# Second parts of the weights on VectorE in the first mixing, and fixed places for the sums in the second

## The chip, the core and the metric

The kernel runs on one core of a Trainium2 chip. The metric is the device time of one execution in microseconds (us): the median of several runs. A profile of one execution goes with it.

## The reference

One layer of a hybrid decoder is applied to a prompt (2048 tokens) and to 8 short samples (8 tokens each, with states from earlier tokens). Both share the weights; the model width is 1024.

```python
h = rmsnorm(x, norm_mix_w)
rq, rk, rv, rg, hq, hf, hi, hg = split(h @ w_in)              # 8 parts of 4 heads x 128
o_r = retention(rotary(rq), rotary(rk), rv)                    # 4 heads, fixed decay per head
f   = lb + (1 - lb) * sigmoid(hf)                              # 4 heads, decay per channel
o_h = gated_recurrence(silu(hq), 1 - f, hi, log(f))
o   = concat(head_rmsnorm(o_r) * silu(rg), head_rmsnorm(o_h) * silu(hg))
x   = x + o @ w_out
x   = x + square(relu(rmsnorm(x, norm_ffn_w) @ w_up)) @ w_down # inner width 4096
y   = rmsnorm(x, final_norm_w)
```

All values are float32; the states after the last token are outputs too.

## The kernel before

The tokens are worked through in three groups of 512, 832 (the 64 sample tokens and 768 of the prompt) and 768 columns. Each group passes through a mixing (input projection and recurrence of four heads), the output projection and the feed-forward part. "First mixing" is `mix` of group 0, "second mixing" that of group 1. The features lie on the 128 partitions, the tokens along the free dimension.

**Split float32.** TensorE multiplies in a reduced format (fp32r). Each float32 operand is therefore cut in two: a first part `hi`, made on ScalarE by a copy that rounds, and a second part `lo = raw - hi`. A product takes three matmuls: hi x hi, hi x lo, lo x hi.

**Weights.** `plan_stream` lists all weight tiles (128 x 1024) in the order of use. `weight(i)` runs when tile i is needed, and prepares the tiles up to i + 2: it loads `raw` (two buffers) on the SP queue, casts `hi` on ScalarE (line 277) and has `second_part` (line 292) make `lo`. Until the change line 280 chooses the engine: entries of the first 40 tiles, which are those of group 0's input and output projection, go to GpSimd (POOL) at once if their number is over 3 and not a multiple of 4, which are 27 tiles; the others go to VectorE, 4 ticks later. Tiles of the feed-forward part of groups 1 and 2 carry a third field, which chooses the engine there. In group 0, `next_weight` stores both parts in DRAM from tile 4 on (line 325); groups 1 and 2 load these, so they make no second parts in their mixing but for the first four tiles.

**Order of the work.** Instructions are issued by a clock of ticks: a tick follows each step of the matmul loops (`tick`). `later(n, f)` issues f n ticks on. The mixer of a head (`mixer`) is such a list of ticks: logs, scans, then for six widths the exponents (lines 832, 833 on POOL), their exponential (line 837 on ScalarE) and the decayed queries and keys (843, 844 on VectorE); scores in PSUM that are copied into a tile `AT` (lines 857, 877, 900 on VectorE, 916 on ScalarE); retention scores (lines 970, 971); column sums (504, 505) of parts cut by lines 359 and 360; transposes (788, copied by 790 and 792). Projections leave PSUM through lines 639 and 702 on VectorE. Small PSUM tiles share four buffers named `mm`, the projections' two named `pj`. The framework also orders instructions of one engine by when their operands are ready.

**Heads.** In group 1 a head's projections take 4 x 24 ticks, its values 56, and the gates of a head 2 x 24, the gates coming ahead of the next head's projections or at the end. So the mixer of a head starts after ticks 96, 296, 496 and 696 of the mixing, and the mixing ends after tick 800. The output projection takes 192 ticks more.

**Sums of weights.** The feed-forward part of groups 1 and 2 multiplies 2 x 2 blocks by seven products instead of eight and so needs sums of weight blocks. `plan_sums` makes them on the side: a set loads four tiles (A21, A22, A11, A12, tag `sum`, four buffers) at 0, 0, 12 and 24 ticks from its start, makes four additions on VectorE (line 1293) at 40, 50, 60 and 70, and stores the results at 60, 70, 80 and 90 (line 1298). Seven sets (for w_up) are made in group 0's feed-forward part, eight (for w_down) in the second mixing. What is left of them is issued by a loop `while self.side`. Their loads and stores, like all DMAs named here, are on the SP queue.

Of the kernel before, what the change touches and what calls it, by code (L numbers as in the profile page):

```python
# [41 lines left out]
W_UP0 = W_OUT0 + N_OUT  # L42
W_DN0 = W_UP0 + N_UP
NQ = FF // (4 * P)
NO = NQ // 2
# [162 lines left out]
class Kernel:  # L208
# [43 lines left out]
    def weight(self, i):  # L252
        n = len(self.stream)
        while self.w_next < min(i + 1 + self.ahead, n):
            j = self.w_next
            e = self.stream[j]
            if e[0] == "p":

                self.wts[j] = tuple(self.wp.tile([P, WT], F32R, tag=tag, name=tag) for tag in ("hi", "lo"))
                for part, kept in zip(self.wts[j], self.kept[e[1]]):  # L260
                    self.nc.sync.dma_start(part.bitcast(F32), kept)
                self.w_next += 1
                self.w_load = max(self.w_load, j + 1)
                continue
            while self.w_load <= j or j >= self.n_first and self.w_load <= j + 2 and self.w_load < n:
                if self.stream[self.w_load][0] == "p":
                    break
                k, later = self.w_load, self.w_load >= self.n_first
                raw = self.raws[k] = self.wp.tile([P, WT], F32, tag="sum" if later and k % 3 else "raw", name="raw",
                                                  bufs=4 if later and k % 3 else 2)  # L270
                e = self.stream[k]
                self.fetch(raw, self.sums[e[1]] if e[0] == "s" else self.I["w"][e[1]])
                self.w_load += 1
            raw = self.raws.pop(j)
            hi = self.wp.tile([P, WT], F32R, tag="hi", name="hi")
            lo = self.wp.tile([P, WT], F32R, tag="lo", name="lo")
            self.nc.scalar.copy(hi, raw)  # L277
            self.wts[j] = (hi, lo)
            self.second[j] = raw
            pool = self.stream[j][2] if len(self.stream[j]) > 2 else j % 4 and 3 < j < W_UP0  # L280
            if pool or j < 4:
                self.second_part(j, self.nc.gpsimd if pool else self.nc.vector)
            else:
                self.later(4, self.second_part, j, self.nc.vector)
            self.w_next += 1
        self.second_part(i, self.nc.vector)
        return self.wts[i]
# [91 lines left out]
    def build(self):  # L379
        nc, tc, I = self.nc, self.tc, self.I  # L380
        with ExitStack() as ctx:
            cp = ctx.enter_context(tc.tile_pool(name="cp", bufs=1))
            self.wp = ctx.enter_context(tc.tile_pool(name="wp", bufs=3))
            self.sl = ctx.enter_context(tc.tile_pool(name="sl", bufs=NSLAB))
            self.ld = ctx.enter_context(tc.tile_pool(name="ld", bufs=NLD))
            self.small = ctx.enter_context(tc.tile_pool(name="small", bufs=2))
            self.pj = ctx.enter_context(tc.tile_pool(name="pj", bufs=2, space=bass.MemoryType.PSUM))
            self.pm = ctx.enter_context(tc.tile_pool(name="pm", bufs=4, space=bass.MemoryType.PSUM))
            self.dp = ctx.enter_context(tc.tile_pool(name="dp", bufs=1, space=bass.MemoryType.DRAM))
            self.w_next = self.w_load = self.w_use = 0  # L390
            self.n_mm = self.n_ticks = 0
            self.raws, self.sums, self.side = {}, {}, deque()
            self.ordered, self.spread, self.n_proj = True, False, 0
            self.ahead = 2
            self.wts, self.second, self.kept = {}, {}, {}
            self.blocks = deque()
            self.plan_stream()

            con = cp.tile([P, NCONST], F32, name="con")
            vec = cp.tile([P, NVEC], F32, name="vec")  # L400
            msk = cp.tile([P, 2 * NLV, P], U8, name="msk")
            self.ones = cp.tile([P, P], F32, name="ones")
            self.ones_r = cp.tile([P, P], F32R, name="ones_r")
            nc.vector.memset(self.ones, 1.0)
            nc.vector.tensor_copy(self.ones_r, self.ones)
            eps = cp.tile([P, 2], F32, name="eps")
            nc.vector.memset(eps[:, 0:1], EPS)
            nc.vector.memset(eps[:, 1:2], EPS * DK)
            self.eps, self.eps_h = eps[:, 0:1], eps[:, 1:2]
            self.con, self.vec, self.msk = con, vec, msk  # L410
            self.ident = con[:, C_ID:C_ID + P]

            gs = []
            off = 0
            for ns, p0, n in GROUPS:
                g = type("G", (), {})()
                g.i, g.ns, g.p0, g.n, g.T, g.off = len(gs), ns, p0, n, ns + n, off
                off += g.T
                nch = n // C
                first = nch // 2  # L420
                g.pieces = [(0, g.T)] if g.T <= 512 else [(0, g.T // 2), (g.T // 2, g.T)]
                g.segs = [list(range(first)), list(range(first, nch))]
                gs.append(g)
            nc.scalar.dma_start(vec, I["vec"])
            nc.scalar.preload_act_table_set("natural_log_exp_and_others")
            self.norm_in(gs[0], True)
            self.ahead = 2
            self.weight(0)

            self.reset = cp.tile([P, P + NS], F32, name="reset")  # L430
            nc.gpsimd.memset(self.reset, 1.0)
            nc.gpsimd.memset(self.reset[:, P:].rearrange("p (c t) -> p c t", t=SLEN)[:, :, 0:1], 0.0)
            self.S = cp.tile([P, 2 * H, P], F32, name="S")
            self.AT = [cp.tile([P, 3, P], F32, name=f"AT{i}") for i in range(2)]
            for a in self.AT:
                nc.gpsimd.memset(a, 0.0)
            self.ATs = cp.tile([P, P], F32, name="ATs")
            nc.gpsimd.memset(self.ATs, 0.0)
            self.lower_bounds(cp)

            sums = [(("u", t), W_UQ0 + 4 * t) for t in range(1, NQ)]
            sums += [(("d", o, v), W_DQ0 + 4 * (2 * o + v)) for o in range(NO) for v in range(2)]
            for i, g in enumerate(gs):
                nxt = gs[i + 1] if i + 1 < len(gs) else None
                if i == 0:
                    self.mix(g)
                    self.plan_sums(sums[:NQ - 1], 90, 200)

                    self.spread = True
                    self.out_proj_first(g)  # L450
                    self.ffn_first(g, nxt)
                    self.spread = False
                    continue
                if i == 1:
                    self.finish_first(gs[0])
                    self.plan_sums(sums[NQ - 1:], 100, 84)
                else:
                    self.finish(gs[i - 1])
                self.mix(g)
                while self.side:  # L460
                    self.side.popleft()[1]()
                self.out_proj(g)
                self.ffn(g, nxt)
            nc.sync.dma_start(self.O["ret_p"].rearrange("h d v -> d h v"), self.S[:, :H])
            nc.sync.dma_start(self.O["hg_p"].rearrange("h d v -> d h v"), self.S[:, H:])
# [814 lines left out]
        self.later(4 * KB + 10, factor)  # L1280


    def plan_sums(self, sets, first, every):
        nc, w = self.nc, self.I["w"]
        self.side = deque()

# [10 lines left out]
            s = self.sums[key + (name,)] = self.dp.tile([P, WT], F32, name="s" + "".join(map(str, key)) + name)  # L1297
            self.tc.keep_in_program_order(nc.sync.dma_start(s, x[name]))

        for j, (key, i) in enumerate(sets):  # L1300
            x, t = {}, self.n_ticks + first + every * j
            steps = [(0, load, x, i, "A21", "A22"), (12, load, x, i, "A11"), (24, load, x, i, "A12"),
                     (40, make, x, "S1", "A21", ALU.add, "A22", "A22"),
                     (50, make, x, "S3", "A11", ALU.subtract, "A21", "A21"),
                     (60, make, x, "S2", "S1", ALU.subtract, "A11", "A11"),
                     (70, make, x, "S4", "A12", ALU.subtract, "S2", "A12")]
            steps += [(d, keep, x, key, name) for d, name in ((60, "S1"), (70, "S3"), (80, "S2"), (90, "S4"))]
            for d, fn, *a in sorted(steps, key=lambda z: z[0]):
                self.side.append((t + d, lambda fn=fn, a=a: fn(*a)))
# [463 lines left out]
```

## Time and profile before

| what | value |
|---|---|
| median of 3 runs | 2588.03 us (2586.77 to 2589.51) |
| profiled execution, its own time | 2586.12 us |
| its span, first to last instruction | 2584.3 us |
| mean granted TensorE clock | 0.997 |
| DMA | 442.33 MB, mean 171 GB/s |
| first mixing | about 30 to 300 us |
| second mixing | about 680 to 1110 us |

The profile's lines give engine (PE is TensorE, PEld its weight loads, DVE is VectorE, ACT ScalarE, POOL GpSimd), line of the kernel, operation, names of the tiles written and read, and times. In a timeline, the bracket at the end of a row is the time for which the engine was idle before it, and the instruction that ended the wait.

### The profile page before, as it was taken

The page shows a single profiled execution, that of the slowest core. Times are in us where ns is not written, and L with a number is a line of the kernel's source. Part 1 is how long each engine was busy: PE and PEld are TensorE (multiplying, and loading weights), DVE is VectorE, ACT ScalarE, POOL GpSimd, SP SyncE. Part 2 cuts the span into 40 slices and gives each one's busy share as a digit, 9 for nine tenths or more (in the row PEclk, how much of TensorE's full clock was granted, in tenths as well). Part 3 has the DMA queues.
Part 4 walks back from the last instruction along what each step waited for, and adds up shares of the span by engine and source line. Part 5 has one row for each costly group of instructions (what it writes and reads, how often), then busy time and mean ns, then how long its engine had stood idle before and what let it go on. Part 6 is the DMA issues. An engine that isn't in the chain of part 4 may idle for free. (4 is left out here: it accounts for less than half of the span.)

```text
span 2584.3 us, 37190 instructions
## 1 busy us (share of the span) xinstructions
PE 2538.6 (98%) x14689; PEld 2404.1 (93%) x14689; DVE 1688.4 (65%) x2122; ACT 1166.5 (45%) x1575; POOL 772.3 (30%) x480
## 2 busy tenths in 40 slices
PE   8999999999999999999999999999999999999997
PEld 6888788888999999999999999999999999999997
DVE  6666776556666576646655977875556465559886
ACT  6666533234434343345434444454444354345443
POOL 5655251111234143201222322242244012223222
PEclk9999999999999999999999999999999999999999
DMA  7556755554264655613456555442222325565452
GB/s 256 207 201 210 279 202 195 192 195 161 98 220 158 225 202 170 230 72 136 167 169 228 206 174 177 149 160 82 99 108 100 120 90 179 183 218 194 171 180 82
DMA packets 146237, 442.33 MB, mean 171 GB/s; under 512 B 14736, under 2 KB 36240, under 8 KB 146064
## 3 DMA queue, kind: packets, MB, share of 16 engines
q1 hardware_dynamic: 145920, 439.94, 48.8%
q8 instruction: 116, 1.90, 0.3%
q14 instruction: 57, 0.47, 0.1%
q10 hardware_dynamic: 144, 0.02, 0.0%
HBM read 331.11 MB, written 108.79 MB: 170 GB/s over the span
## 5 line engine op out<-in xcount | busy, mean ns | idle before, releaser
L352 PE MATMUL pj<-slab,hi 128*128 128x416 f32 (+2 forms) x2844 | 742.4, 364 | 6.3 <-ACT hi L277 5.9
L277 ACT CAST hi<-raw 128x1024 fp32r<-128x1024 f32 x330 | 346.7, 1051 | 677.9 <-PE pu L1145 191.6
L292 POOL TENSOR_TENSOR lo<-raw,hi 128x1024 fp32r<-128x1024 f32 x119 | 314.7, 2645 | 933.9 <-ACT hi L277 866.4
L352 PEld LDWEIGHTS pj<-slab,hi 128*128 128x128 f32 x2844 | 514.3, 189 | 39.1 <-ACT hi L277 5.9
L1145 PE MATMUL pd<-slab,hi 128*128 128x416 f32 (+1 forms) x1792 | 469.5, 342 | 5.1 <-DVE slab L1588 3.1
L352 PE MATMUL pj<-slab,lo 128*128 128x416 f32 (+2 forms) x1422 | 435.6, 364 | 0.1
L1145 PE MATMUL pu<-slab,hi 128*128 128x416 f32 (+1 forms) x1600 | 408.1, 342 | 0.0
L292 DVE TENSOR_TENSOR lo<-raw,hi 128x1024 fp32r<-128x1024 f32 x211 | 269.5, 1277 | 188.7 <-ACT hi L277 188.2
L1145 PEld LDWEIGHTS pd<-slab,hi 128*128 128x128 f32 x1792 | 329.4, 188 | 8.7 <-DVE slab L1588 3.7
L1145 PE MATMUL pd<-slab,lo 128*128 128x416 f32 (+1 forms) x896 | 307.9, 344 | 0.0
L1145 PEld LDWEIGHTS pu<-slab,hi 128*128 128x128 f32 x1600 | 294.0, 188 | 1.5
L352 PEld LDWEIGHTS pj<-slab,lo 128*128 128x128 f32 x1422 | 259.9, 189 | 17.2 <-issue 1.9
L1145 PE MATMUL pu<-slab,lo 128*128 128x416 f32 (+1 forms) x800 | 264.2, 343 | 0.0
L352 PE MATMUL mm<-slab,hi 128*128 128x512 f32 x740 | 229.5, 390 | 0.0
L727 PE MATMUL pjv<-hi,slab 128*128 128x256 f32 x1088 | 211.9, 286 | 1.0 <-ACT slab L737 1.0
L1344 DVE TENSOR_TENSOR slab<-slab 128x832 fp32r<-128x832 f32 (+1 forms) x144 | 162.9, 1148 | 37.4 <-ACT slab L1340 18.1
L727 PEld LDWEIGHTS pjv<-hi,slab 128*128 128x128 f32 x1088 | 174.2, 190 | 3.0 <-ACT slab L737 1.4
L1340 ACT CAST slab<-slab 128x832 fp32r<-128x832 f32 (+1 forms) x144 | 122.0, 860 | 116.7 <-DVE slab L1351 83.1
L1145 PEld LDWEIGHTS pd<-slab,lo 128*128 128x128 f32 x896 | 168.1, 188 | 0.5
L352 PEld LDWEIGHTS mm<-slab,hi 128*128 128x128 f32 x740 | 138.5, 188 | 29.2 <-ACT slab L1175 0.4
L727 PE MATMUL pjv<-lo,slab 128*128 128x256 f32 x544 | 153.8, 283 | 0.0
L1145 PEld LDWEIGHTS pu<-slab,lo 128*128 128x128 f32 x800 | 149.7, 188 | 0.5
(205 smaller groups left out, 3708.3 us busy)
## 6 DMA issues: line engine op xcount, KB each, us to landing
raw<-w SPq DMA_DIRECT2D x270, 512.0 KB, 4.1
u<-ld SPq DMA_DIRECT2D x32, 416.0 KB, 4.2
slab<-u SPq DMA_DIRECT2D x32, 416.0 KB, 5.7
u<-ld SPq DMA_DIRECT2D x32, 384.0 KB, 4.6
slab<-u SPq DMA_DIRECT2D x32, 384.0 KB, 4.9
ld<-x SPq DMA_DIRECT2D x16, 416.0 KB, 4.8
ld<-x SPq DMA_DIRECT2D x16, 384.0 KB, 4.0
raw<-su1S SPq DMA_DIRECT2D x8, 512.0 KB, 3.9
```

The costliest lines, as they stand in the source:

```text
L277: self.nc.scalar.copy(hi, raw)
L292: eng.tensor_tensor(out=lo, in0=self.second.pop(j), in1=hi.bitcast(F32), op=ALU.subtract)
L352: self.nc.tensor.matmul(pj[:, i, :T2], w, a[:, c0:c1], start=j == 0 and q == 0, stop=j == n - 1 and q == 2)
L727: nc.tensor.matmul(pj[:, i * 256:(i + 1) * 256], a[:, s:s + C], ww, start=kb == 0 and q == 0, stop=kb == KB - 1 and q == 2)
L1145: self.nc.tensor.matmul(*a, **k)
L1340: self.nc.scalar.copy(hi[:, :g.T], B[name][:, :g.T])
L1344: self.nc.vector.tensor_tensor(out=lo[:, :g.T], in0=B[name][:, :g.T], in1=hi.bitcast(F32)[:, :g.T], op=ALU.subtract)
```

## The change

In the first mixing, all second parts of weights are made on VectorE, 4 ticks after their cast; no tile of the first 40 goes to POOL. `plan_sums` takes a list of starts instead of a first start and a distance. The starts of the seven sets for w_up are the same as before (90 + 200 j). Those of the eight sets for w_down were 100 + 84 j; now they are 141, 226, 341, 426, 541, 626, 741 and 826, two in each stretch of 200 ticks. In groups 1 and 2 the output projection now comes ahead of the loop that issues what is left of the sums.

```diff
-            pool = self.stream[j][2] if len(self.stream[j]) > 2 else j % 4 and 3 < j < W_UP0
+            pool = len(self.stream[j]) > 2 and self.stream[j][2]
...
-                    self.plan_sums(sums[:NQ - 1], 90, 200)
+                    self.plan_sums(sums[:NQ - 1], [90 + 200 * j for j in range(NQ - 1)])
...
-                    self.plan_sums(sums[NQ - 1:], 100, 84)
+
+                    self.plan_sums(sums[NQ - 1:], [141 + 200 * (j // 2) + 85 * (j % 2) for j in range(2 * NO)])
                 else:
                     self.finish(gs[i - 1])
                 self.mix(g)
+                self.out_proj(g)
                 while self.side:
                     self.side.popleft()[1]()
-                self.out_proj(g)
                 self.ffn(g, nxt)
...
-    def plan_sums(self, sets, first, every):
+    def plan_sums(self, sets, starts):
...
-        for j, (key, i) in enumerate(sets):
-            x, t = {}, self.n_ticks + first + every * j
+        for start, (key, i) in zip(starts, sets):
+            x, t = {}, self.n_ticks + start
```

## Prediction

> **What bounds the kernel now.** I read the page first, for the engine shares.
>
> ```profile
> span 2584.3 us, 37190 instructions
> PE 2538.6 (98%) x14689; PEld 2404.1 (93%) x14689; DVE 1688.4 (65%) x2122; ACT 1166.5 (45%) x1575; POOL 772.3 (30%) x480
> ```
>
> TensorE is busy 98% of the span. Neither half of the change touches a matmul, so it can only act through the 45.7 us in which TensorE is not busy, or by making more of them. Next I read TensorE's waits in the first mixing (30 to 300 us); columns are the total, the times and the longest. Those of the second mixing stand further down, one by one.
>
> ```profile
> PE mm L970 <- ACT AT L916: 7.6, 3, 3.5
> PE mm L913 <- DVE slab L971: 3.0, 1, 3.0
> PE mm L505 <- DVE slab L360: 2.5, 2, 1.8
> PE mm L788 <- DVE slab L1005: 1.7, 1, 1.7
> ```
>
> So 7.6 us of the first mixing end on ScalarE's copies into AT (line 916) and 7.2 us on VectorE. The view of windows adds what the clock did at the stalls (the columns after the stretch are busy time of PE, PEld, DVE, ACT, POOL, then PEclk, DMA share, GB/s).
>
> ```profile
> 30.00:300.00 270.00, 254.88 (x1528) 217.72 (x1527) 172.97 (x316) 167.69 (x273) 150.19 (x111) 0.98 0.64 220
> 57.83:61.24 3.41, 3.41 (x22) 1.92 (x20) 0.81 (x3) 0.78 (x3) 1.28 (x1) 0.50 0.95 370
> 119.45:122.86 3.41, 3.41 (x28) 2.45 (x29) 1.60 (x6) 1.39 (x4) 1.28 (x1) 1.00 0.93 316
> 180.71:184.12 3.41, 3.41 (x17) 2.24 (x16) 1.23 (x5) 0.41 (x2) 1.27 (x1) 0.50 1.02 395
> 245.57:248.98 3.41, 3.20 (x15) 2.66 (x16) 2.30 (x7) 2.76 (x6) 1.21 (x1) 0.50 0.80 327
> ```
>
> Three times the granted clock was 0.50 for 3.41 us right at a stall, once (119 us) it stayed at 1.00. It granted 22, 17 and 15 matmuls instead of 28 there; I take it that a stretch at half clock costs half of itself, 1.7 us.
>
> **First mixing: 27 second parts leave POOL.** The timeline shows what makes the 7.6 us (start, duration, engine and line, in brackets the idle time before and who ended it). This is the second head; its first line is the exponents' predecessor on POOL.
>
> ```profile
> 111.20 0.83 POOL L833 TENSOR_TENSOR slab<-slab 128x256 f32<-128x256 f32 x1
> 112.60 1.03 ACT L277 CAST hi<-raw 128x1024 fp32r<-128x1024 f32 x1
> 113.71 2.52 POOL L292 TENSOR_TENSOR lo<-raw,hi 128x1024 fp32r<-128x1024 f32 x1 [1.68 <-ACT hi L277]
> 113.90 2.60 DVE L844 TENSOR_TENSOR slab<-slab 128x256 f32<-128x256 f32 x1
> 114.26 1.04 ACT L277 CAST hi<-raw 128x1024 fp32r<-128x1024 f32 x1
> 116.43 1.63 DVE L292 TENSOR_TENSOR lo<-raw,hi 128x1024 fp32r<-128x1024 f32 x1
> 116.94 1.64 POOL L833 TENSOR_TENSOR slab<-slab 128x256 f32<-128x256 f32 x1
> 118.62 0.63 ACT L837 ACTIVATE slab<-slab 128x512 f32<-128x512 f32 x1 [3.32 <-POOL slab L833]
> 119.16 0.40 ACT L916 COPY AT<-mm 64x128 f32<-64x128 f32 x2
> 119.45 0.71 PE L970 MATMUL mm<-slab 128*128 128x128 f32 x4 [2.02 <-ACT AT L916]
> ```
>
> POOL works in order. From 112.03 us it waits 1.68 us for ScalarE's cast, spends 2.52 us on the second part, and only then comes to the exponents (lines 832, 833). ScalarE's exponential (line 837) waits 3.32 us for them, the copies to AT queue behind it, and TensorE wants the PSUM buffer that these copies free. The other two stalls have the same chain:
>
> ```profile
> 51.59 2.52 POOL L292 TENSOR_TENSOR lo<-raw,hi 128x1024 fp32r<-128x1024 f32 x1 [1.68 <-ACT hi L277]
> 52.14 1.05 ACT L277 CAST hi<-raw 128x1024 fp32r<-128x1024 f32 x1
> 57.15 0.71 PE L970 MATMUL mm<-slab 128*128 128x128 f32 x4 [3.53 <-ACT AT L916]
> 180.46 1.02 PE L970 MATMUL mm<-slab 128*128 128x128 f32 x4 [2.01 <-ACT AT L916]
> ```
>
> Without the second part, POOL goes on to the exponents at 112.03 and ends both by 113.7 (2 x 0.83). What is late next is ScalarE: its second cast ends at 115.30, the exponential at 115.93, and the first copy 0.29 later (119.45 - 119.16), at 116.2. TensorE would have started at 119.45 - 2.02 = 117.43: no stall. At 180 us the same. In the first head the cast ends at 53.19, the copy at 54.1, against 57.15 - 3.53 = 53.62: about 0.5 us stay. **Term A: 3.53 + 2.02 + 2.01 - 0.5 = 7.0 us won.** The half clocks at 57.8 and 180.7 go with their stalls. **Term B: 2 x 1.7 = 3.4 us won.**
>
> On the clock, the Trainium skill (TensorE: Matmul & The Clock Gate, "What's actually happening") says that the clock halves after an idle window of about 3.4 us. The trace agrees for the 3.53 us stall but not for the 2.01 us one, which halved it too while 2.02 us at 119 us did not; by the page only 1.7 us would be won, and the sum would end 1.7 us higher.
>
> **Second mixing: the sums move.** A set's four additions come 40 to 70 ticks after its start. A head takes 200 ticks here, and its mixer starts at ticks 96, 296, 496 and 696. The old starts, 84 apart, put additions 12 to 32 ticks behind such a start at ticks 308 to 328 and 506, and 32 to 62 behind at 728 to 758. The view of the second mixing shows TensorE's stalls right behind these (the additions run in order, so the one at 810 us, the ninth, is that of tick 308):
>
> ```profile
> 810.37 1.84 DVE L1293 TENSOR_TENSOR raw<-raw 128x1024 f32<-128x1024 f32 x1
> 813.85 0.47 PE L505 MATMUL mm<-slab,ones_r 128*128 128x448 f32 x1 [1.63 <-DVE slab L360]
> 817.52 1.85 DVE L1293 TENSOR_TENSOR raw<-raw 128x1024 f32<-128x1024 f32 x1
> 823.61 0.91 PE L970 MATMUL mm<-slab 128*128 128x128 f32 x6 [1.12 <-DVE AT L877]
> 916.87 1.84 DVE L1293 TENSOR_TENSOR raw<-raw 128x1024 f32<-128x1024 f32 x1
> 920.35 0.47 PE L505 MATMUL mm<-slab,ones_r 128*128 128x448 f32 x1 [1.63 <-DVE slab L360]
> 1045.57 2.13 DVE L1293 TENSOR_TENSOR raw<-raw 128x1024 f32<-128x1024 f32 x1 [0.94 <-DMA raw<-w]
> 1049.31 0.33 PE L788 MATMUL mm<-con,slab 128*128 128x128 f32 x1 [1.43 <-ACT slab L792]
> ```
>
> The four stalls are 1.63 + 1.12 + 1.63 + 1.43 = 5.8 us. The new starts put them 85 to 115 and 170 to 200 ticks behind it, in every head. Old additions stood at 96 to 126 and at 180 to 200 (ticks 392 to 422, 476 to 496), and no stall of TensorE followed them. The last one, at 200, falls on the next mixer's start:
>
> ```profile
> 908.25 1.22 DVE L1293 TENSOR_TENSOR raw<-raw 128x1024 f32<-128x1024 f32 x1
> 910.22 1.03 DVE L702 TENSOR_TENSOR slab<-pj,ld 128x832 f32<-128x832 f32 x1 [0.75 <-ACT slab L646]
> ```
>
> That is exactly such an addition, and VectorE still idled 0.75 us before the eviction. Stretched to 1.84 us it would fit barely; I allow 0.2 us in each of three heads. **Term D: 5.8 - 0.6 = 5.2 us won.**
>
> The last set now ends at tick 916, where the mixing ends at 800, and the output projection now comes ahead of the loop that empties the rest. Its four additions, four loads and four stores pass to the output projection (ticks 800 to 992), on SP beside the loads of kept weights. Those are asked for two weights (48 ticks) ahead, which hides them; with that cover gone, the four additions' 4 x 1.22 = 4.9 us. All stores are out before tick 944, when the first raw weight of the feed-forward wants a buffer. The first list of starts (90 + 200 j) gives the old values: nothing.
>
> **First mixing: what the 27 cost on VectorE.**
>
> ```profile
> L292 POOL TENSOR_TENSOR lo<-raw,hi 128x1024 fp32r<-128x1024 f32 x27 | 66.6, 2466 | 80.9 <-ACT hi L277 79.2 <-DVE AT L877 1.7
> L292 DVE TENSOR_TENSOR lo<-raw,hi 128x1024 fp32r<-128x1024 f32 x8 | 11.8, 1470 | 3.4 <-ACT hi L277 3.4
> SPq L241 <- POOL lo L292: 63.4, 27, 4.1
> L1293 DVE TENSOR_TENSOR raw<-raw x32: 1197/1218/3009, 729.5 to 1050.2; 128x1024 f32<-128x1024 f32 x32
> ```
>
> The second parts already there took 1.47 us each; an addition of the same size in the second mixing took 1.22 us (median). I take 1.22, since less of POOL is in their way: 27 x 1.22 = 33 us. They will wait for ScalarE's cast as the eight do, 3.4 x 27/8 = 11 us. VectorE has 270 - 173 = 97 us idle there, so it does not become the bound by amount; some time also comes back (line 844 took 2.60 us beside the POOL operation). But behind each waiting second part stand VectorE's PSUM evictions and splits, and TensorE waits for those (lines 360, 971). The nearest row is the second mixing: 32 additions of this size led to stalls of 5.8 us, 0.18 us each. **Term C: 27 x 0.18 = 4.9 us lost.** Its bounds: all of 33 us on TensorE's path, or below nothing, since the 7.2 us that end on VectorE, with the half clock at 245.6 us (1.7 us), could go as VectorE is no longer held up by POOL: -8.9.
>
> The load of a weight waits on SP for the second part two weights back, as it has two buffers (63.4 us in 27 waits, off TensorE's path); copies of finished weights queue behind it. On VectorE the second part takes 1.2 us less, so the load starts earlier unless VectorE is more than that behind. I put this at nothing; if it fails, ScalarE's cast is late, which is part of C's upper bound.
>
> **Sum.** A + B - C + D: 7.0 + 3.4 - 4.9 + 5.2 = 10.7 us won. The profiled execution took 2586.1 us, 1.9 under the median of the runs, and would come to 2575.4; the median, 2588.0, to 2577.3.
>
> **Rivals.** *The shared work keeps its order (first mixing gives nothing).* VectorE's second part at 116.43 ran beside line 833 on POOL, which took 1.64 us instead of 0.83. If two second parts on VectorE hold the exponents as long as POOL's own did, and C eats the rest, A, B and C cancel: 2588.0 - 5.2 = 2582.8. Against it: one such hold is 0.8 us, two are 1.6, under the 3.3 us that ScalarE now waits. The Trainium skill says this too (Perfetto Trace Analysis, "Optimizing Scalar/DVE Operations"): GpSimd and VectorE share an SBUF port, so moving operations between them might not help. Chance 0.15.
>
> *VectorE's order becomes the limit (slower).* Each second part stands, waiting for its cast, ahead of an eviction that TensorE needs. If all 33 us reach TensorE: 2588.0 - 7.0 - 3.4 - 5.2 + 33 = 2605.4. It decides from 15.6 + 5.2 = 20.8 us on, 0.77 us of each 1.22. For it: the stall at 245.8 us lies in a pile-up on VectorE. Against: 97 us idle. Chance 0.06.
>
> *The sums only move their stalls.* If each head has its stall at the new places, D is nothing: 2577.3 + 5.2 = 2582.5. Against it the 908 us row. Chance 0.09.
>
> *POOL was not the cause.* If ScalarE's casts set the AT copies, A and B stay, C is paid: 2588.0 + 4.9 - 5.2 = 2587.7. Against it the 3.32 us wait. Chance 0.06.
>
> **How the numbers follow.** The forecast has 0.64. Two tenths of a per cent, 5.2 us, is about what a measurement of this kernel can tell from no change, so faster means under 2582.8 and slower over 2593.2. The first and third rivals lie at that bound; I split them. Faster: 0.64 + 0.075 + 0.045 = 0.76; same: 0.12 + 0.06 = 0.18; slower 0.06. The range reaches up to 2586, over the first and third rivals; above it lie 0.12. Down, without C and the allowances (A 7.6, B 3.4, D 5.8) the median is 2571.3, and half of C's gain of 8.9 us leads to 2567.
>
> **What would show it.** Right: no wait of line 970 for line 916 over 0.6 us in the first mixing; the clock at 1.00 near 57 and 180 us; line 292 on POOL gone before 300 us; line 844 near 0.41 us there; no wait of line 505 near 814 and 920 us. Wrong: line 970 still waiting, with the exponents early (then ScalarE), or new waits of lines 352, 505 or 913 for VectorE of more than 5 us in the first mixing, or waits of line 505 at each head of the second.

## The result and the profile after

The changed kernel takes 2564.66 us (median of 5 runs, 2564.37 to 2567.08), the kernel before 2586.77 us beside it (2586.33 to 2589.51). The ratio is 0.9912, 95% interval [0.9901, 0.9922]: faster by 22.1 us, where 10.7 were forecast and the range ended at 2567.

In the changed kernel, lines from 456 on carry a number one higher (970 is 971 and so on). The page after:

```profile
span 2563.0 us, 37181 instructions
PE 2533.7 (99%) x14689; PEld 2401.2 (94%) x14689; DVE 1694.3 (66%) x2149; ACT 1165.0 (45%) x1575; POOL 706.9 (28%) x453
```

VectorE is busy only 6 us longer though it took over 27 operations, and POOL 65 us shorter. TensorE's waits in the first mixing after (total, times, longest):

```profile
PE mm L914 <- DVE slab L972: 1.3, 1, 1.3
PE mm L506 <- DVE slab L360: 0.5, 1, 0.5
PE pj L352 <- ACT slab L738: 0.4, 1, 0.4
PE mm L971 <- ACT AT L917: 0.2, 1, 0.2
```

The 7.6 us that ended on the copies to AT are 0.2; the 7.2 us that ended on VectorE are 1.8. The windows show the clock at 1.00, over the whole first mixing and at the time of the first old stall:

```profile
30.00:282.00 252.00, 249.62 (x1526) 214.67 (x1525) 182.30 (x342) 166.13 (x273) 84.52 (x84) 1.00 0.69 238
57.00:61.00 4.00, 4.00 (x24) 3.42 (x24) 3.41 (x5) 3.94 (x6) 1.48 (x2) 1.00 1.01 407
```

The timeline of the second head, at the place shown before:

```profile
105.86 0.85 POOL L834 TENSOR_TENSOR slab<-slab 128x256 f32<-128x256 f32 x1
107.25 1.21 DVE L292 TENSOR_TENSOR lo<-raw,hi 128x1024 fp32r<-128x1024 f32 x1
107.37 1.04 ACT L277 CAST hi<-raw 128x1024 fp32r<-128x1024 f32 x1
108.31 0.63 ACT L838 ACTIVATE slab<-slab 128x512 f32<-128x512 f32 x1
108.84 0.41 ACT L917 COPY AT<-mm 64x128 f32<-64x128 f32 x2
109.05 0.41 DVE L845 TENSOR_TENSOR slab<-slab 128x256 f32<-128x256 f32 x1
109.39 1.21 DVE L292 TENSOR_TENSOR lo<-raw,hi 128x1024 fp32r<-128x1024 f32 x1
109.78 0.61 PE L971 MATMUL mm<-slab 128*128 128x128 f32 x4
```

POOL is through with the exponents (now line 834) at 106.71, before the casts are. ScalarE does the exponential straight behind its second cast, with no wait in brackets, the copies follow, and line 971 starts without a wait. The two second parts take 1.21 us each on VectorE, and line 845 takes 0.41 us where it took 2.60.

TensorE's waits in the second mixing after, and the timeline at the longer one:

```profile
PE pjv L728 <- ACT slab L738: 1.9, 4, 0.6
PE mm L774 <- DVE slab L771: 1.1, 1, 1.1
```

```profile
1050.98 1.21 DVE L1294 TENSOR_TENSOR raw<-raw 128x1024 f32<-128x1024 f32 x1
1053.11 1.21 DVE L1294 TENSOR_TENSOR raw<-raw 128x1024 f32<-128x1024 f32 x1
1054.25 1.28 DVE L771 TENSOR_TENSOR slab<-slab,con 128x512 f32<-128x512 f32 x2
1055.07 1.96 PE L774 MATMUL mm<-slab 128*128 128x512 f32 x4 [1.07 <-DVE slab L771]
```

All four old stalls are gone; one new one stands behind two additions of the seventh set, ahead of the sample states of the last head.

Where the time came from is read best from TensorE's matmuls in order: both kernels have 14689. After 1800 of them, well behind the first mixing, the next starts at 342.2 us before and 324.3 after: 17.9 us won. After 6200, behind the second mixing, it starts at 1124.3 and 1102.9: 21.4 us, so 3.6 in the second mixing. Nothing changes behind that, so the new place of the output projection cost nothing. The stalls account for the 17.9: 7.4 us at line 970, 5.4 us on VectorE and, at the prediction's 1.7 us for a stretch, 5.1 us of half clock (three stretches of 3.41 us before, none after).

### The profile page after: what moved, and what is told of

Its sections match the earlier page's. It is cut to its first block, busy times and chain, and to the rows that moved or that the text cites. A ratio compares the mean times of both kernels' runs of the same rounds, so it can differ in the third digit from the quotient of the medians.

```text
span 2563.0 us, 37181 instructions
## 1 busy us (share of the span) xinstructions
PE 2533.7 (99%) x14689; PEld 2401.2 (94%) x14689; DVE 1694.3 (66%) x2149; ACT 1165.0 (45%) x1575; POOL 706.9 (28%) x453
## 5 line engine op out<-in xcount | busy, mean ns | idle before, releaser
L292 POOL TENSOR_TENSOR lo<-raw,hi 128x1024 fp32r<-128x1024 f32 x92 | 248.0, 2696 | 852.0 <-ACT hi L277 779.3
L292 DVE TENSOR_TENSOR lo<-raw,hi 128x1024 fp32r<-128x1024 f32 x238 | 301.6, 1267 | 198.2 <-ACT hi L277 197.8
```

Source lines behind the costliest of these rows:

```text
L292: eng.tensor_tensor(out=lo, in0=self.second.pop(j), in1=hi.bitcast(F32), op=ALU.subtract)
```

## The experiments

Each kernel was timed side by side with the kernel before; the difference in us is the ratio applied to 2588 us. Where a kernel is compared with the changed one, it goes by these differences (the changed kernel: -22.8, [-25.6, -20.2]). An edit shifts the line numbers behind it: line 970 is 972 in pool_after and pool_behind, 973 in no_seconds and 974 in pool_twin and dve_twice.

| kernel | median us | ratio, 95% interval | difference us |
|---|---|---|---|
| first_half | 2571.22 | 0.9934 [0.9919, 0.9948] | -17.1 |
| second_half | 2582.85 | 0.9983 [0.9974, 0.9992] | -4.4 |
| four_tiles | 2577.11 | 0.9952 [0.9936, 0.9969] | -12.4 |
| other_23 | 2580.82 | 0.9975 [0.9965, 0.9984] | -6.5 |
| pool_late | 2588.70 | 1.0002 [0.9993, 1.0012] | +0.5 |
| pool_after | 2587.70 | 0.9996 [0.9987, 1.0005] | -1.0 |
| pool_behind | 2582.81 | 0.9978 [0.9968, 0.9987] | -5.7 |
| pool_twin | 2599.58 | 1.0050 [1.0034, 1.0067] | +12.9 |
| pool_fill | 2591.04 | 1.0015 [1.0005, 1.0024] | +3.9 |
| dve_twice | 2576.25 | 0.9958 [0.9943, 0.9972] | -10.9 |
| no_seconds | 2566.10 | 0.9913 [0.9896, 0.9929] | -22.5 |
| no_adds | 2564.15 | 0.9903 [0.9889, 0.9916] | -25.1 |
| earlier | 2566.39 | 0.9912 [0.9898, 0.9925] | -22.8 |

**The two parts, each alone.** first_half is the kernel before with the first line of the diff; second_half has all the rest.

> Only the first part of the change: all second parts of the first 40 tiles on VectorE, the sums where they were. If the two parts add, as the two traces say (17.9 us of the 21.4 us are won by the end of the first mixing), 17.9 us under the kernel before, and the granted clock at 1.00 throughout the first mixing. Rival, the second part also counts for more than its stalls: 12 us or less here.

> Only the second part: new starts of the sums, output projection ahead of the loop. If the parts add: 3.6 us under the kernel before, with the stalls of lines 505, 970 and 788 in the second mixing gone. Rival as in the other run: 8 us or more.

-17.1 us [-21.0, -13.5] and -4.4 us [-6.7, -2.1]: the parts add up to the whole. In first_half the clock stays at 1.00 throughout the first mixing. In second_half the four stalls are gone, and the same new one as in the changed kernel stands at 1075 us.

**Which second parts.** The timelines before showed one second part per head ahead of the exponents: those of tiles 7, 15, 23 and 31 (their stores stand beside them on SP).

```diff
-            pool = ... else j % 4 and 3 < j < W_UP0
+            pool = ... else j % 4 and 3 < j < W_UP0 and j not in (7, 15, 23, 31)   # four_tiles
+            pool = ... else j in (7, 15, 23, 31)                                   # other_23
```

> The kernel before with only four of the 27 second parts on VectorE, those of tiles 7, 15, 23 and 31, which stand in POOL's queue ahead of exponents that TensorE soon needs. Theory (position in POOL's queue): these four carry the three stalls of line 970 (7.6 us) and the half clocks behind them (3.4 us), perhaps the one at 245 us too (1.7 to 4 us): 10 to 14 us under the kernel before. Rival (POOL's total work, or its share of the port): in proportion, 4/27 of 17.9 us, 2.7 us.

> The reverse: the other 23 second parts on VectorE, tiles 7, 15, 23 and 31 stay on POOL. Theory (position): the three stalls of line 970 stay, and 4 to 8 us are won, those of VectorE's stalls at 45, 266 and 268 us. Rival (total work): 23/27 of 17.9 us, 15 us.

four_tiles wins 12.4 us [8.0, 16.6]: four operations of 27 bring most of the first part's gain (after 1800 matmuls 10.4 us in its trace, 16.2 in that of first_half). Its waits in the first mixing:

```profile
PE mm L505 <- DVE slab L360: 2.4, 2, 1.6
PE mm L913 <- DVE slab L971: 1.9, 1, 1.9
PE mm L788 <- DVE slab L1005: 1.7, 1, 1.7
...
PE mm L970 <- ACT AT L916: 0.2, 1, 0.2
```

Line 970 no longer waits; of VectorE's stalls those of lines 505 and 788 are as before (2.5 and 1.7), that of line 913 is 1.9 us instead of 3.0. These are what the other 23 carry. other_23 wins 6.5 us, inside the theory's span, but not by its way: the stalls of line 970 went there too, although POOL still waits 1.68 us for the cast ahead of the exponents in every head. TensorE had stopped earlier, at matmuls that read lo and waited for VectorE (3.7, 1.3, 1.3 and 1.3 us). The order on the engines is not that of before, so this run does not test the theory.

**The place in POOL's queue.** Three kernels keep all 27 second parts on POOL and issue them later: pool_late all 27 by 12 ticks, pool_after the four tiles by 36, pool_behind the four by 47.

```diff
-            if pool or j < 4:
+            if j in (7, 15, 23, 31):
+                self.later(47, self.second_part, j, self.nc.gpsimd)                                      # pool_behind
+            elif pool or j < 4:
```

> The kernel before, with the 27 second parts on POOL but issued 12 ticks later. If their place ahead of the exponents made the three stalls of line 970, these go or move and 5 to 10 us are won, though POOL's work and its hold on VectorE stay. If POOL's amount of work counts: within 3 us of the kernel before.

> The kernel before, but the second parts of tiles 7, 15, 23 and 31 are issued 36 ticks later, still on POOL: behind the exponents that the copies to AT need, and ahead of the tile's use. POOL's work and its port are as before. Theory (these four stand ahead of the exponents in POOL's queue): the three stalls of line 970 go, 8 to 12 us are won, unless a second part comes late for its own tile (then a stall of a matmul that reads lo). Rival (POOL's amount of work): within 3 us of the kernel before.

> The kernel before, with the second parts of tiles 7, 15, 23 and 31 issued 47 ticks later, still on POOL. At 12 and 36 ticks the order on POOL stayed as it was, because the exponents of the fourth width are issued after 45; at 47 three of the four (7, 15 and 23) stand behind them. POOL's work and its port are as before. Theory (place in POOL's queue): the three stalls of line 970 go, 7.6 us, and the half clocks behind two of them with them: 8 to 12 us under the kernel before; a stall of a matmul that reads lo may take some of it back. Rival (amount of POOL's work): within 3 us.

pool_late and pool_after change nothing: the order of POOL's instructions is that of before, so neither theory was tried. (The change also issues the second parts 4 ticks later than before; by pool_late a delay alone wins nothing.) pool_after's timeline is still the old one:

```profile
113.70 2.52 POOL L294 TENSOR_TENSOR lo<-raw,hi 128x1024 fp32r<-128x1024 f32 x1 [1.68 <-ACT hi L277]
118.61 0.63 ACT L839 ACTIVATE slab<-slab 128x512 f32<-128x512 f32 x1 [3.32 <-POOL slab L835]
119.44 0.71 PE L972 MATMUL mm<-slab 128*128 128x128 f32 x4 [2.00 <-ACT AT L918]
```

The exponents that come too late are issued at tick 45. At 47 three of the four stand behind them (pool_behind, the second head):

```profile
110.46 1.03 ACT L277 CAST hi<-raw 128x1024 fp32r<-128x1024 f32 x1
110.61 0.84 POOL L835 TENSOR_TENSOR slab<-slab 128x256 f32<-128x256 f32 x1
111.62 2.40 POOL L294 TENSOR_TENSOR lo<-raw,hi 128x1024 fp32r<-128x1024 f32 x1 [0.17 <-POOL slab L835]
113.06 0.64 ACT L839 ACTIVATE slab<-slab 128x512 f32<-128x512 f32 x1
113.54 0.61 PE L972 MATMUL mm<-slab 128*128 128x128 f32 x4
```

The exponents run while ScalarE casts, the second part follows without the 1.68 us of waiting, and line 972 does not wait. Its total in the first mixing is 0.3 us instead of 7.6, with as much work on POOL as before (148.5 us between 30 and 300, against 150.2), and the half clocks at 57 and 180 us are gone. So the place made these stalls, not the amount. The kernel wins 5.7 us [3.4, 8.3], under the 8 to 12 expected. Counted matmul by matmul, its trace wins 10.3 us at the three places, where the changed kernel wins 10.6, and gives 3.6 us back between the heads: 1.2 us in three new waits of line 1039 for VectorE, 0.5 in two of line 858 for ScalarE's cast, the rest not itemized. In the second mixing 2.0 us more went, where line 790 stalls 1.9 us instead of 1.4 and a half clock follows.

**POOL's load put back.** pool_twin is the changed kernel with the old operation again on POOL, into a tile that nobody reads; pool_fill has three memsets there.

```diff
+            if j % 4 and 3 < j < W_UP0:
+                junk = self.wp.tile([P, WT], F32, tag="sum", name="junk", bufs=4)
+                self.nc.gpsimd.tensor_tensor(out=junk, in0=raw, in1=hi.bitcast(F32), op=ALU.subtract)   # pool_twin
+                for _ in range(3):                                                                      # pool_fill
+                    self.nc.gpsimd.memset(junk, 0.0)
```

> The changed kernel, and on POOL, at the places where its 27 second parts stood, the same operation again into a tile that nobody reads. VectorE keeps all second parts. If POOL's hold on the exponents and on VectorE's operations with two SBUF inputs made the stalls, they come back: 13 to 20 us over the changed kernel, line 970 waiting for line 916 again, single operations of line 844 over 2 us. If the gain came from anything else (the order of the instructions, weights loaded earlier): within 3 us of the changed kernel.

> The changed kernel, and on POOL three memsets of 128 x 1024 for each of the 27 tiles (about 0.95 us each by the 0.79 us of 832 columns, 2.9 us in sum, more than the 2.47 us of a second part); they read no SBUF. If POOL's time alone counts, the exponents are late again and 8 us or more are lost. If the reading port counts, VectorE's operations stay at their short times and under 5 us are lost. The memsets need no cast, so they may run earlier than the second parts did.

pool_twin loses all that was won and 12.9 us more, 36 us against the changed kernel, where 13 to 20 were expected. Its waits in the first mixing, and its timeline in the second head:

```profile
PE mm L974 <- ACT AT L920: 9.7, 3, 3.7
PE po L1041 <- DVE AT L949: 4.7, 3, 1.6
PE mm L917 <- DVE slab L975: 4.4, 1, 4.4
```

```profile
120.38 1.23 DVE L295 TENSOR_TENSOR lo<-raw,hi 128x1024 fp32r<-128x1024 f32 x1 [0.32 <-ACT hi L277]
120.42 3.41 POOL L283 TENSOR_TENSOR junk<-raw,hi 128x1024 f32<-128x1024 f32 x1 [1.68 <-ACT hi L277]
121.86 2.26 DVE L847 TENSOR_TENSOR slab<-slab 128x256 f32<-128x256 f32 x1
```

Each engine holds the other: POOL takes 3.41 us instead of 2.4 beside VectorE's second part, and then VectorE 2.26 us instead of 0.41. The old stalls are back and longer.

pool_fill loses 27 us against the changed kernel, and all of it in the first 100 us: the memsets wait for no cast, ran early (none between 95 and 277 us), and stood in front of the start's norm (a wait of 10.5 us) and the first head. By the 400th matmul, at 107 us, it was 25.6 us behind, and stayed there. So POOL's queue counts by itself, but these memsets did not stand where the second parts did. What it shows is how VectorE fares beside them:

```profile
68.50 3.63 POOL L284 MEMSET junk<- 128x1024 f32 x4
69.10 1.21 DVE L296 TENSOR_TENSOR lo<-raw,hi 128x1024 fp32r<-128x1024 f32 x1
70.57 0.41 DVE L848 TENSOR_TENSOR slab<-slab 128x256 f32<-128x256 f32 x1
```

Both operations take their shortest times in the middle of POOL's memsets. All nine second parts that ran wholly beside memsets took 1.21 to 1.23 us.

**What the second parts cost VectorE.** dve_twice makes each of the 27 twice; no_seconds makes none of them.

```diff
+            if j % 4 and 3 < j < W_UP0:                                                              # dve_twice
+                eng.tensor_tensor(out=lo, in0=raw, in1=hi.bitcast(F32), op=ALU.subtract)
...
+            skip = j % 4 and 3 < j < W_UP0                                                           # no_seconds
+            lo = hi if skip else self.wp.tile([P, WT], F32R, tag="lo", name="lo")
```

> The changed kernel with each of the 27 second parts made twice on VectorE, 27 x 1.22 = 33 us more on that engine in the first mixing. By the predicted price (0.18 us each) 4.9 us over the changed kernel. If VectorE has room for them: within 2 us. If VectorE is near its limit: 10 us or more.

> The changed kernel without the 27 second parts (the first part stands in for them in the matmuls and in the stores, so the weights lose their low bits): POOL relieved and VectorE not loaded. It splits the predicted term C. If VectorE's new work costs what the prediction said, 4.9 us under the changed kernel, as far as its 2.4 us of stalls in the first mixing allow: so 2 to 3 us under it. If the new work costs nothing: within 1 us. In both cases the stalls of lines 505, 913 and 788 at 45, 246, 267 us of the kernel before are at most as long as in the changed kernel, if POOL's hold on VectorE made them.

In no_seconds the first part is used in place of the second, so these weights count about twice, rather than lose their low bits as the expectation says; the work of TensorE is the same. It is as fast as the changed kernel (-22.5 [-26.9, -18.4] against -22.8); at the 1800th matmul it had won 17.4 us, the changed kernel 17.9. Its waits and its window in the first mixing:

```profile
PE mm L916 <- DVE slab L974: 0.8, 1, 0.8
PE mm L973 <- ACT AT L919: 0.3, 1, 0.3
PE pj L354 <- ACT slab L740: 0.2, 1, 0.2
```

```profile
30.00:282.00 252.00, 250.48 (x1529) 215.32 (x1528) 149.83 (x316) 167.52 (x274) 78.27 (x84) 1.00 0.68 238
```

VectorE is busy 149.8 us there and 182.3 in the changed kernel: 32.5 us of second parts that cost nothing that these runs can tell, though 1.0 us of VectorE's stalls (1.8 against 0.8) goes with them. The relief from POOL alone took 6.4 of VectorE's 7.2 us of stalls away. Its size shows in VectorE's other work, which is what is left of its busy time without second parts: 161.2 us before (173.0 less 11.8), 140.0 in no_seconds (149.8 less 9.8) and 138.8 in the changed kernel (182.3 less 43.5). So VectorE took on 32 us and got 22 back. One place before, where four scans took 3.56 us beside a second part on POOL and TensorE waited:

```profile
40.21 2.85 POOL L292 TENSOR_TENSOR lo<-raw,hi 128x1024 fp32r<-128x1024 f32 x1
40.72 3.56 DVE L817 TENSOR_TENSOR_SCAN slab<-reset,slab 128x128 f32<-128x128 f32 x4
44.91 0.39 PE L505 MATMUL mm<-slab,ones_r 128*128 128x256 f32 x1 [1.77 <-DVE slab L360]
```

The same place in the changed kernel, with the second part on VectorE:

```profile
40.44 1.22 DVE L292 TENSOR_TENSOR lo<-raw,hi 128x1024 fp32r<-128x1024 f32 x1
41.58 1.36 DVE L818 TENSOR_TENSOR_SCAN slab<-reset,slab 128x128 f32<-128x128 f32 x4
43.58 0.39 PE L506 MATMUL mm<-slab,ones_r 128*128 128x256 f32 x1 [0.51 <-DVE slab L360]
```

A second dose is not free: dve_twice stands 11.9 us behind the changed kernel, 0.44 us for each of the 27. Most of it shows: VectorE's stalls are 6.4 us longer, and 6.8 us of half clock come with the longest one, at 240 us:

```profile
PE mm L917 <- DVE slab L975: 4.8, 4, 3.0
PE po L1041 <- DVE AT L949: 1.2, 3, 0.5
```

**The additions at their new places.** no_adds leaves the 32 additions out; earlier moves the seventh set.

```diff
+            if len(sets) == NQ - 1:                                                                  # no_adds
...
-... [141 + 200 * (j // 2) + 85 * (j % 2) for j in range(2 * NO)]
+... [141 + 200 * (j // 2) + 85 * (j % 2) - 20 * (j == 6) for j in range(2 * NO)]                         # earlier
```

> The changed kernel without the 32 additions of the second mixing (the loaded blocks are stored as the sums, so the computation lacks these sums); loads and stores stay. It shows what the additions still cost at their new places. By the stall in the trace at 1055 us (1.1 us behind two additions) 1 to 2 us under the changed kernel; if the waits of line 728 for line 738 at each head (1.9 us in sum) come from them too, 2 to 3 us.

> The changed kernel with the seventh set of the second mixing 20 ticks earlier (721 instead of 741), so that its last two additions do not stand ahead of the sample states' products at 1055 us. The stall of 1.1 us there goes; 1 us under the changed kernel, too little to be measured in the total, so the trace is to show it. If another stall takes its place: no gain.

no_adds shows no difference that these runs can tell (-25.1 [-28.7, -21.7]). In its trace the stall at 1055 us is gone, and with it 1.6 us that the changed kernel gives back around that place, counted matmul by matmul; the four waits for line 738 stay: they are not the additions' doing. In earlier the stall stays (1.06 us at 1053 us): the last two additions, 20 ticks earlier, delay the same chain on VectorE, one of them stretched to 3.00 us. So this set is not mended by 20 ticks, and no version here that does all the work beats the changed kernel.

## Why the prediction was wrong, by its own steps

The direction, the mechanism of line 970's stalls and the end of the four stalls in the second mixing were right. The size was not, because one term had the wrong sign. The signs that the prediction named for being right came; the one that bears on term C, line 844 near 0.41 us, had been given no price.

- **Term C failed, in sign.** The step was: "The nearest row is the second mixing: 32 additions of this size led to stalls of 5.8 us, 0.18 us each. Term C: 27 x 0.18 = 4.9 us lost." The runs put a gain of 5.4 us in its place: VectorE's stalls fell from 7.2 to 1.8 us. no_seconds shows that the 27 cost about 1 us of stalls in the traces, nothing that the total can tell, and that the relief from POOL is the term; four_tiles, with 23 still on POOL, keeps 6.0 us of them. The row of line 844 (2.60 us beside POOL) stood in the prediction and was called "some time also comes back"; its weight, 22 us of VectorE's time, was not worked out, and the value was taken from another stage. The bound of -8.9 us held, but the range went only half way to it: the runs used 7.1 of it (5.4 and the third half clock).
- **Term B was short by one stretch.** Forecast 3.4 us for two, and three went, 5.1 us by the same price: the third half clock, at 245.6 us, went with the stall of line 913, which fell from 3.0 to 1.3 us. The prediction had it only in C's bound. The price itself was somewhat high: 1.2 to 1.6 us a stretch, as the last section shows.
- **Term A**: 7.0 forecast, 7.4 measured. pool_behind shows its cause, the place in POOL's queue. The 0.5 us that the first head was to keep were 0.2.
- **Term D**: 5.2 forecast, 3.6 measured. The four stalls went, and up to the 5800th matmul 5.2 us were won in the second mixing. Then a stall of 1.1 us came behind the seventh set, and 1.6 us went back. Those additions stand 85 to 115 ticks behind the mixer's start, where the prediction, from the row of another head, expected no stall; it looked for new ones at the next head's start. In the first three heads none came at that place. The waits for line 738, which the additions do not cause, rose from 1.0 to 1.9 us. (A slip without weight: tick 506 is 10 behind the mixer's start, not 12.)
- **Sum**: 7.4 + 5.1 + 5.4 + 3.6 = 21.5, against the spans' 2584.3 - 2563.0 = 21.3. With 1.2 to 1.6 us for each half clock it is 20.0 to 21.2; what is left is not itemized.
- **Rivals.** That the first mixing gives nothing, and that POOL was not the cause, are refuted by first_half and pool_behind. The slower case did not come; but dve_twice shows that its mechanism begins with the next 27 operations. That the sums only move their stalls holds for one of four.

The Trainium skill's remark (Perfetto Trace Analysis, "Optimizing Scalar/DVE Operations") that moving work between GpSimd and VectorE might not help does not fit here: one operation takes 2.40 us on POOL and 1.22 us on VectorE (medians), and the move won 17 us.

## What to carry to other kernels

Ask of an operation on a slow in-order engine what stands behind it: four of 27 operations made most of the loss, by standing ahead of short ones that a chain to TensorE needed. When work leaves an engine whose operations stretch those of another, count what the other gets back before pricing what it takes on. A price per operation from another stage is no price here: the first 27 cost nothing that could be measured, the next 27 cost 0.44 us each.

## What the runs showed of the hardware

**POOL's reads, not its activity, hold VectorE.** VectorE's second parts took 1.21 to 1.23 us amid POOL's memsets, which read no tile (pool_fill). Single operations of 0.41 us took 2.26 (pool_twin) and 2.60 us (before) beside a POOL operation that reads two tiles, and ended 0.3 us after it. The Trainium skill (SBUF — State Buffer, "SBUF: two separate sides") says that a VectorE operation with two SBUF inputs and a GpSimd operation that reads SBUF lock each other out for a whole instruction; these traces agree.

**The same stalls cost different amounts of clock.** Four profiles have the same stalls in the first mixing (3.5, 2.0, 2.0 and 2.9 to 3.0 us). Half clock was granted there for 10.2 us (before), 13.7 (second_half), 10.2 (pool_late) and 6.8 us (pool_after), always in multiples of 3.41. In second_half, three such stretches follow the first stall:

```profile
56.53:66.77 10.24, 8.73 (x38) 6.63 (x39) 2.96 (x7) 5.72 (x11) 4.91 (x6) 0.50 0.81 298
```

The 2.0 us stalls brought one only in the kernel before, at 180 us. In the second mixing one stall of 1.9 us (line 788) stands in six profiles; a half clock follows it in four_tiles, pool_late and pool_behind, and none in first_half, other_23 and pool_after. The price shows where two traces differ in nothing else: the three kernels without the stretch at 180 us win 1.5 us there on the kernel before, and after the first stall one stretch more costs pool_late 1.6 us, two more cost second_half 2.5. A stall of 2 us thus costs 2 us or 3.5; what decides it, no run shows. It may be part of why runs of the kernel before spread over 2585 to 2593 us, which was not tried.

**A later issue counts only once it passes another.** Moving the second parts' issue by 12 or 36 ticks left their place on POOL as it was; at 47 ticks, past the exponents' own issue at 45, the order changed.
